# Stores of split weights: from SyncE's DMA queue to GpSimd's

## The chip, the cores and the metric

The kernel runs as one program on one core of a Trainium2 chip. The metric is the device time of that core in microseconds (us). Three timed runs of the kernel before gave 2495.51, 2503.52 and 2504.46 us; the median is 2503.52 us. The profiled execution, a fourth one, took 2499.25 us, of which 2496.5 us are the span that the trace covers.

Engines go by their short names: PE is the matrix engine (PEld its weight loads), DVE the vector engine, ACT the scalar engine, POOL is GpSimd, SP is SyncE, which here only issues DMAs. "SPq" or "POOLq" means the instruction queue of that engine.

## The reference, cut to what matters

One layer of a decoder trunk is run on a prompt of 2048 tokens and on 8 single-token samples, model width 1024:

```python
h    = rms_norm(x) * (1 + sc1) + sh1
proj = h @ w_in                       # 1024 x 3080: q, k, v, gate z, beta, alpha, u, vb
mix  = concat(gated_delta(q, k, v), u * (W_s @ vb + b))
x    = x + g1 * (mix @ w_out)         # 1024 x 1024
h2   = rms_norm(x) * (1 + sc2) + sh2
up   = causal_dwconv(h2 @ w_up)       # 1024 x 5632
x    = x + g2 * ((silu(up[:2816]) * up[2816:]) @ w_down)   # 2816 x 1024
y    = rms_norm(x)
```

All is in float32. What counts here is that the four weight matrices w_in, w_out, w_up and w_down are each used once per block of tokens, so each is needed several times.

## The kernel before, in words

**Split weights.** Each float32 operand of a large matmul is split in two parts (`split`, L98 to L100): ACT copies it to a float32r tile (the high part), DVE subtracts that from the original (`sub_lo`, L97: the low part). `gemm_steps` makes three matmuls per pair (L119 to L121). A block of split weights is a tile of 128 x 2 x 512 (512 KB).

**Kept blocks.** `wblock` (L159) gets a tile w and, the first time that a block is needed, the raw weights. Then it splits them into w and stores w to a DRAM buffer of its own (`kept[key]`, store at L166). Each later time it loads the split block from there (L162, on POOL's queue), with no split. The first time is the first 512 tokens of the mixer (segment 0: 24 tiles of w_in with 2 blocks each, and 8 of w_out with 2) and the first third of the FFN's tokens (22 pairs of w_up with 7 blocks each, 22 rows of w_down with 2). That is 48 + 16 + 154 + 44 = 262 stores of 512 KB, 198 of them in the FFN. All further blocks are loads.

**Raw weights** come in by SP's queue: `wslab` (L153) for w_in, w_out and w_up, L1058 in `down_weights` for w_down. They share SP's queue with the stores, the w_mod slabs, the token blocks (L917, L694, L725) and the output (L1128). A tile is taken from a pool: tag "w" has 6 buffers for raw slabs and split blocks of mixer and w_down, "wb" has 6 for split blocks of w_up, and "S" has 2 for raw w_down halves and for the sums of w_up blocks. A buffer can be filled again when its last readers are done; for a split block these are the matmuls and the store.

**Mixer** (to about 1046 us): four segments of 512 tokens. Segment 0 has also the w_mod matmuls and the samples. POOL has a few memsets there.

**FFN**: three chunks of 688, 688 and 680 tokens. The loop goes over 22 pairs. `up_pair` makes seven products per pair (a Strassen-like form) and adds them: six on DVE, and on POOL `G.tensor_tensor u` (L1034) and the `add` behind it (L1035, recorded at L1009). DVE reads u next (L1007/L1009 for the last product), ACT reads the sum in the convolution (L1014), DVE finishes it (L1021). After 2 or 3 pairs (`ROUNDS`) a *down round* begins: `down_weights` fetches the rows of w_down, `down` multiplies, and DVE adds the result into xa (L1086, L1087), which frees the PSUM bank.

**Order.** Each engine and each DMA queue works through its list in order; an instruction that waits for a semaphore holds up all behind it. The lists are laid out at build time by the framework's planner, which plays the whole program with assumed durations and puts on each engine whatever can go, the earlier in the program first. So when a DMA changes its queue, all lists are laid out anew.

Of the kernel before, what the change touches and what calls it, by code (L numbers as in the profile page):

```python
# [9 lines left out]
F32 = mybir.dt.float32  # L10
# [35 lines left out]
def trunk(ctx, tc, A, O):  # L46
    nc = tc.nc
    V, S_, G, PE = nc.vector, nc.scalar, nc.gpsimd, nc.tensor
# [50 lines left out]
    def split(out_h, out_l, a, eng=None):  # L99
        S_.activation(out=out_h, in_=a, func=AF.Copy)  # L100
        sub_lo(out_l, a, out_h, eng)
# [53 lines left out]


    kept = {}

    def wblock(key, w, src=None):  # L159

        if key in kept:
            G.dma_start(out=w, in_=kept[key])  # L162
        else:
            split(w[:, 0], w[:, 1], src)
            kept[key] = dr.tile([128, 2, 512], F32, name="kept_" + "_".join(map(str, key)))
            nc.sync.dma_start(out=kept[key], in_=w.bitcast(F32))  # L166
        return [(w[:, 0, k * 128:(k + 1) * 128], w[:, 1, k * 128:(k + 1) * 128]) for k in range(4)]

    def wpt():
# [2 lines left out]
    def weight(name, i):  # L172

        raw = None if (name, i, 0) in kept else wslab(A[name][i])
        return [p for j in range(2) for p in wblock(
            (name, i, j), wpt(), None if raw is None else raw[:, j * 512:(j + 1) * 512])]
# [788 lines left out]
    def up_weights(i):  # L965
        names = ("B11", "B21", "T1", "T2", "B22", "T3", "T4")
        block = lambda n, src=None: wblock(("w_up", i, n), wqt(), src)
        if ("w_up", i, "T4") in kept:
            return {n: block(n) for n in names}
        r1, r2 = wslab(A["w_up"][i]), wslab(A["w_up"][FT + i])  # L970
        a11, a12, a21, a22 = r1[:, 0:512], r1[:, 512:], r2[:, 0:512], r2[:, 512:]
        st = lambda: q1.tile([128, 512], F32, tag="S", name="S", bufs=2)
        s1, s2 = st(), st()
        V.tensor_tensor(out=s1, in0=a21, in1=a22, op=ALU.add)
        w = {"B11": block("B11", a11)}
        w["B21"] = block("B21", a12)
        w["T1"] = block("T1", s1)
        V.tensor_tensor(out=s2, in0=s1, in1=a11, op=ALU.subtract)
        w["T2"] = block("T2", s2)
        s4 = st()  # L980
        V.tensor_tensor(out=s4, in0=a12, in1=s2, op=ALU.subtract)
        w["B22"] = block("B22", s4)
        s3 = st()
        V.tensor_tensor(out=s3, in0=a11, in1=a21, op=ALU.subtract)
        w["T3"] = block("T3", s3)
        w["T4"] = block("T4", a22)
        return w
# [62 lines left out]
    def down_weights(i0, m):  # L1050

        w = [[] for _ in range(m)]
        for j in range(2):
            for i in range(m):
                key, raw = ("w_down", i0 + i, j), None
                if key not in kept:
                    raw = q1.tile([128, 512], F32, tag="S", name="S", bufs=2)
                    nc.sync.dma_start(out=raw, in_=A["w_down"][i0 + i][:, j * 512:(j + 1) * 512])  # L1058
                w[i] += wblock(key, wpt(), raw)
        return w  # L1060
# [136 lines left out]
    for s in range(NSEG):  # L1197
# [72 lines left out]
        if s == NSEG - 1:  # L1270
            nc.scalar.dma_start(out=O["nd_p"].rearrange("h k v -> k h v"),
                                in_=state.rearrange("p (h v) -> p h v", h=4))
# [50 lines left out]
    for ci, (c0, W) in enumerate(CB):  # L1323
# [31 lines left out]
        w = down_weights(pend[0], len(pend[1]))  # L1355
# [70 lines left out]
def build(nc, arrays):  # L1426
    A = {n: nc.dram_tensor(f"in_{n}", a.shape, F32, kind="ExternalInput").ap() for n, a in arrays.items()}
    O = {n: nc.dram_tensor(f"out_{n}", s, F32, kind="ExternalOutput").ap() for n, s in _OUTS.items()}
    with tile.TileContext(nc, schedule_with_timeline_sim=True) as tc:
        with ExitStack() as ctx:  # L1430
            trunk(ctx, tc, A, O)
# [11 lines left out]
```

## Time and profile before

| | us |
|---|---|
| median of three runs | 2503.52 |
| profiled execution | 2499.25 |
| its span | 2496.5 |
| PE busy | 2414.7 (97%) |
| DVE busy | 1713.3 (69%) |
| ACT busy | 1045.9 (42%) |
| POOL busy | 501.3 (20%) |

A row of waits reads: engine and line that waited, what ended the wait, total us, times, longest. A row of a timeline reads: start, length, engine, line, operation, output<-input, count, and in square brackets the engine's idle time before it and what ended it; no brackets means no such idle time. A row of windows has for each engine the busy us (and instructions), then the granted share of PE's clock, the busy share of the DMA engines and GB/s.

### The profile page before, as it was taken

To read this page: it belongs to the slowest core of one execution; us is meant where nothing else is said; L and a number is where in the kernel's file an instruction comes from. 1 tells how busy PE (TensorE), PEld (TensorE's weight loads), DVE (VectorE), ACT (ScalarE), POOL (GpSimd) and SP (SyncE) were. 2 spreads that over 40 slices of the span, in tenths; PEclk is the share of its full clock that TensorE was granted. 3 is DMA by queue.
4 is the path that set the end of the run, shared out by engine and by line. 5 is a ranking of instruction groups with operands and counts; after the bars stand their busy time and mean duration, and the time that the engine had idled before them with its cause. 6 is when DMAs were issued, how large, how long until landed. Compare 5 with 4: busy or idle time off the path is not lost.

```text
span 2496.5 us, 41843 instructions
## 1 busy us (share of the span) xinstructions
PE 2414.7 (97%) x15770; PEld 2240.9 (90%) x15770; DVE 1713.3 (69%) x3731; ACT 1045.9 (42%) x2128; POOL 501.3 (20%) x769
## 2 busy tenths in 40 slices
PE   7899999999999999999999999999999999999997
PEld 4798978888887878889999998999999999999997
DVE  4675668455745664799899998766655685666655
ACT  5766655456445645454444444412222242222223
POOL 0000001111201211311111112333333223333333
PEclk9999999999999999999999999999999999999998
DMA  9785787566737754888787778977777778767773
GB/s 377 243 282 170 255 306 212 153 194 202 209 113 223 222 163 143 305 327 307 280 298 295 284 287 302 319 225 237 240 228 223 223 233 296 225 212 231 227 238 116
DMA packets 224057, 600.84 MB, mean 241 GB/s; under 512 B 39345, under 2 KB 67697, under 8 KB 223345
## 3 DMA queue, kind: packets, MB, share of 16 engines
q0 software_dynamic: 84672, 308.32, 39.8%
q1 hardware_dynamic: 128672, 278.83, 31.6%
q10 hardware_dynamic: 10512, 11.04, 1.3%
q8 instruction: 124, 2.03, 0.3%
q14 instruction: 77, 0.62, 0.1%
HBM read 430.39 MB, written 167.70 MB: 240 GB/s over the span
## 4 chain that ended last, share of the span: by engine, by line
PE 75%; DVE 12%; DMA 7%; issue 3%; ACT 2%; SPq 0%; POOL 0%; ACTq 0%; DVEq 0%; POOLq 0%
PE u L119 9%; PE u L120 9%; PE u L121 9%; PE g L119 7%; PE g L120 7%; PE g L121 7%; PE d L119 6%; PE d L120 6%; PE d L121 6%; DVE acc L1021 1%; DVE cv L376 1%; DVE wb L97 1%; DVE sv L508 1%; DMA S<-in_w_down 1%; DVE TP L506 1%
## 5 line engine op out<-in xcount | busy, mean ns | idle before, releaser
L119 PE MATMUL g<-hh,w 128*128 128x512 f32 (+1 forms) x960 | 346.4, 361 | 7.7 <-ACT w L100 7.7
L1021 DVE SCALAR_TENSOR_TENSOR acc<-raw,vec,acc 128x680 f32<-128x680 f32 (+1 forms) x264 | 303.5, 1152 | 70.0 <-ACT acc L1014 67.6
L119 PE MATMUL d<-midh,w 128*128 128x344 f32 (+1 forms) x1008 | 322.2, 325 | 22.1 <-DVE xa L1087 11.9
L119 PE MATMUL u<-T,wb 128*128 128x344 f32 (+1 forms) x1056 | 338.1, 321 | 4.9 <-DMA wb<-kept_w_up_T 2.4
L121 PE MATMUL g<-hh,w 128*128 128x512 f32 (+1 forms) x960 | 341.6, 356 | 0.0
L120 PE MATMUL g<-hl,w 128*128 128x512 f32 (+1 forms) x960 | 340.6, 355 | 0.0
L120 PE MATMUL u<-T,wb 128*128 128x344 f32 (+1 forms) x1056 | 338.4, 321 | 0.3 <-DVE T L97 0.3
L121 PE MATMUL u<-T,wb 128*128 128x344 f32 (+1 forms) x1056 | 337.2, 320 | 0.9 <-DVE wb L97 0.9
L120 PE MATMUL d<-midl,w 128*128 128x344 f32 (+1 forms) x1008 | 323.7, 322 | 0.0
L121 PE MATMUL d<-midh,w 128*128 128x344 f32 (+1 forms) x1008 | 317.4, 322 | 0.4 <-DVE w L97 0.4
L1087 DVE SCALAR_TENSOR_TENSOR xa<-d,mod,xa 128x344 f32<-128x344 f32 (+2 forms) x368 | 206.1, 568 | 153.7 <-PE d L121 144.8
L1014 ACT ACTIVATE acc<-raw,vec 128x680 f32<-128x680 f32 (+1 forms) x132 | 125.9, 956 | 383.7 <-DVE raw L1009 379.1
L119 PE MATMUL u<-B,wb 128*128 128x344 f32 (+1 forms) x792 | 252.6, 320 | 2.7 <-ACT B L100 2.7
L120 PE MATMUL u<-B,wb 128*128 128x344 f32 (+1 forms) x792 | 253.1, 320 | 0.2
L121 PE MATMUL u<-B,wb 128*128 128x344 f32 (+1 forms) x792 | 252.0, 318 | 0.0
L162 POOL DMA_DIRECT2D w<-kept_w_in x144 | 76.2, 529 | 718.0 <-PE g L121 379.4
L119 PEld LDWEIGHTS d<-midh,w 128*128 128x128 f32 x1008 | 191.6, 191 | 26.6 <-issue 11.5
L119 PEld LDWEIGHTS g<-hh,w 128*128 128x128 f32 x960 | 182.9, 191 | 35.1 <-ACT w L100 8.6
L121 PEld LDWEIGHTS g<-hh,w 128*128 128x128 f32 x960 | 182.2, 190 | 28.1 <-issue 2.8
L120 PEld LDWEIGHTS g<-hl,w 128*128 128x128 f32 x960 | 182.9, 191 | 26.7 <-issue 2.0
L119 PEld LDWEIGHTS u<-T,wb 128*128 128x128 f32 x1056 | 199.4, 189 | 6.1 <-DVE sacc L1100 2.1
L121 PEld LDWEIGHTS u<-T,wb 128*128 128x128 f32 x1056 | 199.7, 189 | 1.3 <-DVE wb L97 1.2
(391 smaller groups left out, 5063.4 us busy)
## 6 DMA issues: line engine op xcount, KB each, us to landing
wb<-kept_w_up_T POOLq DMA_DIRECT2D x176, 512.0 KB, 5.0
w<-kept_w_in POOLq DMA_DIRECT2D x144, 512.0 KB, 4.0
wb<-kept_w_up_B POOLq DMA_DIRECT2D x132, 512.0 KB, 4.9
kept_w_up_T<-wb SPq DMA_DIRECT2D x88, 512.0 KB, 4.0
w<-kept_w_down POOLq DMA_DIRECT2D x88, 512.0 KB, 5.0
kept_w_up_B<-wb SPq DMA_DIRECT2D x66, 512.0 KB, 4.1
kept_w_in<-w SPq DMA_DIRECT2D x48, 512.0 KB, 4.2
w<-kept_w_out POOLq DMA_DIRECT2D x48, 512.0 KB, 4.4
```

Of the source, the lines that this page charges most:

```text
L97: (eng or V).tensor_tensor(out=out, in0=a, in1=hi.bitcast(F32), op=ALU.subtract)
L119: PE.matmul(ps[:, :n], wh, mh[:, c0:c0 + n], start=k == ks[0], stop=False)
L120: PE.matmul(ps[:, :n], wh, ml[:, c0:c0 + n], start=False, stop=False)
L121: pe["last"] = PE.matmul(ps[:, :n], wl, mh[:, c0:c0 + n], start=False, stop=k == ks[-1])
L162: G.dma_start(out=w, in_=kept[key])
L376: V.scalar_tensor_tensor(out=acc, in0=cr[:, j:j + SEG], scalar=vc("cqkv", ft * 4 + j), in1=acc, op0=ALU.mult, op1=ALU.add)
L506: V.tensor_tensor(out=tmp, in0=NB[:, j, j + 1:32].unsqueeze(2).to_broadcast([64, r, w]), in1=TB[:, j:j + 1, 0:w].to_broadcast([64, r, w]), ...
L508: V.tensor_tensor(out=TB[:, j + 1:32, 0:w], in0=TB[:, j + 1:32, 0:w], in1=tmp, op=ALU.subtract)
L1014: S_.activation(out=acc[:, off:W], in_=raw[:, 2:2 + m], func=AF.Identity, scale=vc("cffn", ft * 3 + 2), bias=vc("cffb", ft))
L1021: V.scalar_tensor_tensor(out=acc[:, off:W], in0=raw[:, j:j + m], scalar=vc("cffn", ft * 3 + j), in1=acc[:, off:W], op0=ALU.mult, op1=ALU.add)
L1087: V.scalar_tensor_tensor(out=xa[ft][:, b0 + o:b0 + n], in0=ps[:, o:n], scalar=mod[:, 40 + ft, 0:1], in1=xa[ft][:, b0 + o:b0 + n], op0=ALU. ...
```

## The change

The store in `wblock` goes to the queue named in a small dictionary, and that names POOL (`G = nc.gpsimd`) throughout. Raw loads stay on SP, kept loads on POOL.

```diff
     kept = {}
+    keeper = {"q": G}
 
     def wblock(key, w, src=None):
 
@@
         else:
             split(w[:, 0], w[:, 1], src)
             kept[key] = dr.tile([128, 2, 512], F32, name="kept_" + "_".join(map(str, key)))
-            nc.sync.dma_start(out=kept[key], in_=w.bitcast(F32))
+            keeper["q"].dma_start(out=kept[key], in_=w.bitcast(F32))
```

## Rows read from the trace of the kernel before

**Rows 1.** Page: span, and shares of the chain that ended last.
```profile
span 2496.5 us, 41843 instructions
...
PE 75%; DVE 12%; DMA 7%; issue 3%; ACT 2%; SPq 0%; POOL 0%; ACTq 0%; DVEq 0%; POOLq 0%
```

**Rows 2.** Windows: most of segment 0, and the FFN's first chunk (PE, PEld, DVE, ACT, POOL).
```profile
1046.00:1505.00 459.00, 441.04 (x2742) 436.88 (x2741) 429.03 (x866) 208.75 (x336) 61.09 (x43) 0.98 0.81 299
...
60.00:290.00 230.00, 217.36 (x1962) 201.79 (x1960) 154.79 (x453) 155.90 (x390) 0.00 (x0) 0.97 0.69 235
```

**Rows 3.** Waits of PE, 1046 to 1510 us.
```profile
PE d L119 <- DVE xa L1087: 9.9, 6, 2.4
PE d L119 <- ACT w L100: 3.5, 2, 2.4
```

**Rows 4.** Waits of PE, whole run: before the second chunk.
```profile
PE d L119 <- ACT midh L100: 6.0, 2, 5.0
```

**Rows 5.** Waits of PE, 60 to 330 us.
```profile
PE g L119 <- ACT w L100: 7.7, 1, 7.7
```

**Rows 6.** Timeline of ACT at the end of that wait.
```profile
90.12 1.13 ACT L100 ACTIVATE w<-wr 128x512 fp32r<-128x512 f32 x2
```

**Rows 7.** Waits of SP's queue, whole run.
```profile
SPq L166 <- DVE w L97: 179.2, 63, 13.4
...
SPq L166 <- DVE wb L97: 134.6, 91, 3.8
```

**Rows 8.** Timeline of SP's queue, 1300 to 1345 us.
```profile
1305.08 0.32 SPq L166 DMA_DIRECT2D kept_w_up_B<-wb  x1
...
1326.26 0.32 SPq L166 DMA_DIRECT2D kept_w_down<-w  x1
1326.67 0.44 SPq L1058 DMA_DIRECT2D S<-in_w_down  x1
```

**Rows 9.** Waits of ACT, 1046 to 1510 us.
```profile
ACT wb L100 <- PE u L121: 60.2, 40, 4.3
ACT w L100 <- DMA S<-in_w_down: 52.3, 31, 3.3
...
ACT wb L100 <- DMA kept_w_up_B<-wb: 0.5, 1, 0.5
```

**Rows 10.** Instructions on tile kept_w_up_T: ns min/median/max, first and last start.
```profile
L162 POOL DMA_DIRECT2D wb<-kept_w_up_T x176: 527/530/580, 1508.3 to 2443.7; - x176
L166 SPq DMA_DIRECT2D kept_w_up_T<-wb x88: 319/320/1352, 1046.3 to 1505.8; - x88
```

**Rows 11.** Timeline of POOL, one pair of the first chunk.
```profile
1303.23 1.27 POOL L1034 TENSOR_TENSOR mc<-mc 128x344 f32<-128x344 f32 x1 [32.62 <-ACT mc L1033]
1304.46 1.38 POOL L1009 TENSOR_TENSOR raw<-mc 128x344 f32<-128x344 f32 x1
```

**Rows 12.** Timeline of DVE, same pair.
```profile
1301.46 0.69 DVE L97 TENSOR_TENSOR wb<-S,wb 128x512 fp32r<-128x512 f32 x1
...
1303.64 1.41 DVE L97 TENSOR_TENSOR wb<-S,wb 128x512 fp32r<-128x512 f32 x1
1304.97 1.59 DVE L1021 SCALAR_TENSOR_TENSOR acc<-raw,vec,acc 128x680 f32<-128x680 f32 x1
1306.48 0.15 DVE L1007 TENSOR_TENSOR nfs<-u,mc 128x8 f32<-128x8 f32 x1
```

**Rows 13.** Timeline of ACT, same pair.
```profile
1307.28 0.94 ACT L1014 ACTIVATE acc<-raw,vec 128x680 f32<-128x680 f32 x1
```

**Rows 14.** L1021 in the first chunk: ns min/median/max.
```profile
L1021 DVE SCALAR_TENSOR_TENSOR acc<-raw,vec,acc x83: 906/915/1599, 1075.6 to 1504.3; 128x680 f32<-128x680 f32 x83
```

**Rows 15.** Timeline of DVE, one pair of the second chunk.
```profile
1721.53 3.65 DVE L1021 SCALAR_TENSOR_TENSOR acc<-raw,vec,acc 128x688 f32<-128x688 f32 x2 [0.85 <-ACT acc L1014]
```

**Rows 16.** L1021 in the second chunk.
```profile
L1021 DVE SCALAR_TENSOR_TENSOR acc<-raw,vec,acc x88: 921/935/2692, 1562.8 to 1992.8; 128x688 f32<-128x688 f32 x88
```

**Rows 17.** DMA issues: queue, count, size, median us from issue to landing.
```profile
wb<-kept_w_up_T POOLq DMA_DIRECT2D x176, 512.0 KB, 5.0
...
kept_w_up_T<-wb SPq DMA_DIRECT2D x88, 512.0 KB, 4.0
```

## The prediction

> **What bounds the kernel now.** I read the page first, then windows by stage, then the waits of PE in each stage, then the timelines of the queues that the change touches. The chain that ended last is PE for 75%, DVE for 12% and DMA for 7%; SP's and POOL's own queues have 0% [rows 1]. So neither the queue that is relieved nor the one that is loaded stands on the path by itself. They can act only through what they hold up.
>
> The stores run in two places. In segment 0 of the mixer (60 to 290 us) PE is busy 217.4 of 230 us and POOL not at all. In the FFN's first chunk (1046 to 1505 us) PE is busy 441 of 459 us and DVE 429 of 459, so there two engines are nearly full and PE loses only 18 us; POOL is busy 61 us [rows 2]. Of these 18 us, 13.4 lie where a down round begins: 9.9 us wait for the DVE addition into xa that frees a PSUM bank, 3.5 us for ACT's half of a w_down split [rows 3]. At the change to the second chunk PE waits once more, 5.0 us, for ACT's midh [rows 4]. All that a better order of DMAs could give back in the FFN is therefore 18 + 5 = 23 us, 0.9% of the run.
>
> In the mixer the one long wait of PE in reach is 7.7 us before a split of w_in [rows 5]. That split on ACT has no idle time ahead of it [rows 6]: ACT was busy with other work and the raw slab was there, so an earlier load would not move it.
>
> **The change part by part.**
>
> *What goes from SP.* SP's queue stood 179 us in front of stores that waited for DVE's half of a split in w, and 135 us for one in wb [rows 7]. This looks like much, but what is behind such a store? In a down round the queue shows it: the store leaves at 1326.26 us, the next raw load of w_down at 1326.67 us [rows 8]. That load fills one of two S buffers, and the buffer is free only when the same split has read it. Without the store, the load would wait for the same DVE instruction by itself. What goes is the store's issue, 0.41 us a load. From the start of a round to its third block there are two such links, 0.8 us. ACT waits 52 us for raw w_down, in 31 pieces [rows 9], but only 3.5 us of PE's waits end with that split [rows 3]; the others end with DVE, which has a full list there. I take 2 us off, between 0 (DVE is late anyway) and 13.4 us (all round starts come in time). The 64 stores in the mixer: I take 0, since the one wait there isn't for a load [rows 6]; the bound of a gain is that wait, 7.7 us.
>
> *What comes to POOL.* A DMA that POOL issues keeps it busy for 0.53 us, against 0.32 us on SP [rows 10]. 64 x 0.53 = 34 us in segment 0 lie on an empty engine: no cost. 198 x 0.53 = 105 us in the first chunk come to 61 us: 166 of 459 us, no bound. But POOL now waits for each split, and behind a waiting store stand the two additions of each pair. In the pair at 1303 us they start at 1303.23 us and end at 1305.84 us [rows 11]. DVE reads the first one's result at 1306.48 us [rows 12], where it had ended at 1304.50 us, and ACT the second one's at 1307.28 us [rows 13]: a slack of 2.0 and 1.4 us. A store that was already free before (0.53 us) is inside this slack. 22 pairs x 0.53 = 11.7 us is the upper bound for a store that goes first each time and finds no slack; with the slack of the rows I take 1 us.
>
> *What DVE loses beside POOL.* While POOL adds, DVE is longer: L97 takes 1.41 us instead of 0.69 and L1021 1.59 us [rows 12] instead of 0.915 [rows 14], together 1.4 us in this pair. In the second chunk, where POOL issues loads all the time and its additions run back to back, two L1021 take 3.65 us [rows 15] instead of 2 x 0.935 [rows 16], 1.8 us. If the first chunk becomes like the second, that is 0.4 us more a pair, 22 x 0.4 = 9 us of DVE time. PE waits for DVE only at round starts, about one pair in three, so 3 us reach the end. The bounds are -3 us (the additions come to lie beside less DVE work) and 9 us.
>
> *The stores themselves.* POOL's loads of this size land in 5.0 us, SP's stores in 4.0 [rows 17]; a store on POOL isn't in the trace. A split block's buffer is free when its matmuls and its store are done; now ACT waits 60 us for the matmuls and 0.5 us for a landing [rows 9]. So the matmuls are last and cover the store; I take 0.5 us for a landing that is 1 us later; the bound is 1 us at each of those 40 waits on ACT, of which a quarter, 10 us, would reach PE.
>
> *The change to the second chunk.* The first loads of kept w_up blocks and the last 6 stores of w_down now stand in one queue; each store adds 0.53 us, and one may wait for a split. I take 1 us, from -5 us (PE's wait there goes) to +6 us (all of it, twice).
>
> One rule speaks against the change. POOL's loads in the later chunks take 527 to 580 ns with DVE busy beside them [rows 10], so nothing holds up POOL's issue of a DMA there. The Trainium skill, page "SBUF — State Buffer", section "SBUF: two separate sides", says that a DMA issued from GpSimd stands still while certain copies on DVE lock the port through which its descriptors are written. By that rule the stores, issued while DVE is busiest, would be held up for some of DVE's instructions; this is the third rival below.
>
> **Sum.** -2 + 0 + 1 + 3 + 0.5 + 1 = 3.5 us. On the profiled execution, 2499.25 us, that gives 2502.7 us. The median of the runs is 4.3 us above that execution, so I predict 2507 us.
>
> **The rivals.**
>
> *Faster: rounds start in time.* With loads no longer in order with the stores, the planner may put the w_down splits earlier in the lists of ACT and DVE, and the waits at the round starts go. For it: ACT's 31 waits for raw w_down [rows 9]. Against it: two S buffers, and DVE 93% busy. With 13.4 us gone: 2490 us.
>
> *Slower: POOL's additions behind a store that isn't ready.* The place is POOL's queue in each pair. In the pair shown, the next store leaves SP at 1305.08 us [rows 8], after the additions. If the planner puts that store ahead of them, they begin at 1305.08 + 0.53 = 1305.6 instead of 1303.23 us, 2.4 us late; less the slack of 1.4 us, ACT's L1014 and the convolution behind it are 1.0 us late. 22 pairs make 22 us, on DVE and ACT with DVE nearly full: 2526 us. It decides as soon as the planner expects the split before PE's sixth product in most pairs. For it: the lists are made with assumed durations. Against it: in the order of time, as the trace has it, the store comes 1.9 us after.
>
> *Slower: stores held up at issue.* If each of 198 issues were held for one L1021 (0.92 us), POOL would be busy 166 + 182 = 348 of 459 us, and the additions would be 0.9 us late in each pair, 20 us in all: 2524 us. Against it: 580 ns is the longest of 176 loads [rows 10].
>
> **Chances.** My forecast, the queues hardly matter: 0.57, by itself 2494 to 2517 us. Rounds in time 0.20; additions late 0.19; issues held 0.04. A run within 0.5% of 2503.5 us (2491 to 2516 us) can't be told from no change. Faster by more than that: 0.20 for most of the first rival and a bit of the forecast's edge. Slower: 0.23 for the two rivals and 0.04 for the forecast's upper edge, so 0.27. The same: 0.53. The range goes from 2488 us, which leaves out the outer part of the first rival, to 2529 us, past both slow rivals with some of what isn't known of the new lists.
>
> **What would show it.** Right: SP's waits at L166 gone and those at L1058 and L153 grown in their place; PE's waits at the round starts near 13 us; 0.53 us a store on POOL; DVE's L1021 in the first chunk with a maximum over 2 us. Rival one: those PE waits under 5 us. Rival two: POOL's additions start over 1 us after ACT's copy, and DVE or ACT wait for them. Rival three: stores on POOL well over 0.6 us. Wrong altogether: a change of PE's waits in the mixer, or over 10 us at the seams between the stages.

## The result, and the profile after

With all stores on POOL's queue the kernel takes 2517.9 us (median of 5 runs, 2513.8 to 2518.5), beside 2502.3 us for the kernel before (5 runs). The estimated ratio is 1.0069, 95% interval 1.0057 to 1.0082 (the two medians by themselves give 1.0062): slower by 0.6 to 0.7%. In the code after, all lines from 158 on have a number one higher (the store is L167, the load of w_down L1059, the addition into xa L1088).

The page of the kernel after, its span and the first line of its section 4, the chain that ended last:

```profile
span 2512.9 us, 41962 instructions
...
PE 65%; DVE 15%; DMA 10%; issue 5%; ACT 4%; POOL 1%; SPq 0%; DVEq 0%; ACTq 0%; POOLq 0%
```

PE's share fell by 10 points against [rows 1], and DVE, DMA, ACT and the issue of instructions took it. POOL's queue has 0%, but that doesn't clear it: a store's issue counts as POOL, its landing as DMA. Followed through the trace, this chain goes through issues of stores for 4.9 us and through their landings for 14.2 us. Whether POOL's queue brings them onto the path is a question for the experiments. Where the time is lost, the windows tell (the columns of [rows 2]; the mixer's segment 0, then the FFN's first chunk):

```profile
60.00:290.00 230.00, 216.66 (x1956) 201.11 (x1955) 153.06 (x453) 156.06 (x387) 27.75 (x52) 0.98 0.68 232
1046.00:1505.00 459.00, 429.50 (x2635) 423.99 (x2634) 409.34 (x836) 199.19 (x322) 155.06 (x221) 0.97 0.77 288
```

The mixer is as it was. In the first chunk PE and DVE are both less busy than in [rows 2], by 11.5 and 19.7 us, and fewer matmuls fall into the window. Both wait more. POOL is busy 155 us instead of 61, far from full.

From PE's transpose of the row `rtok` that opens the chunk (1053.5 us, before 1056.8) to the matmul that ends PE's wait for midh before the second chunk (1540.1 us, before 1525.3) it takes 486.6 us instead of 468.5: 18.1 us more, which is all of the loss. What lies behind it took 972.8 us instead of 971.2. Two terms make up the 18 us. PE's waits of over 0.2 us in this stretch went from 22.0 to 33.6 us, 11.6 us more. And from 1046 us to 10 us past that matmul, TensorE was granted 1.2 GHz instead of 2.4 for 37.5 us instead of 23.9; PE worked in 33.1 and 20.5 us of these, and half of the difference, 6.3 us, is lost by the slower clock. PE's waits, against [rows 3]:

```profile
PE d L119 <- DVE xa L1088: 19.1, 7, 5.5
PE d L121 <- DVE w L97: 3.0, 3, 1.3
...
PE d L119 <- ACT midh L100: 1.1, 2, 0.9
```

So at the starts of the down rounds PE waits twice as long for DVE's addition into xa. And DVE is not late because it has more to do. Its own waits in the same window, first of the kernel before, then of the one after (us in total, times, longest):

```profile
DVE w L97 <- ACT w L100: 2.1, 5, 0.8
...
DVE wb L97 <- ACT wb L100: 0.2, 1, 0.2
```

```profile
DVE w L97 <- ACT w L100: 16.0, 9, 2.5
DVE wb L97 <- ACT wb L100: 10.7, 9, 3.2
```

DVE stands 26.7 us in front of splits whose ACT half isn't there, where it stood 2.3 us. One round shows how. First DVE after, from the second w_down split of the round to the first addition into xa (start, duration, line, operation, in brackets the idle time before it and what ended it):

```profile
1403.67 0.69 DVE L97 TENSOR_TENSOR w<-S,w 128x512 fp32r<-128x512 f32 x1
1404.28 0.87 DVE L1047 TENSOR_TENSOR acc<-acc 128x688 f32<-128x688 f32 x1
...
1405.14 0.51 DVE L1010 TENSOR_TENSOR raw<-u,mc 128x344 f32<-128x344 f32 x1
1408.18 0.69 DVE L97 TENSOR_TENSOR w<-S,w 128x512 fp32r<-128x512 f32 x1 [2.53 <-ACT w L100]
...
1408.86 0.87 DVE L97 TENSOR_TENSOR midl<-acc,midh 128x688 fp32r<-128x688 f32 x1
1409.69 0.93 DVE L1022 SCALAR_TENSOR_TENSOR acc<-raw,vec,acc 128x680 f32<-128x680 f32 x1
1410.53 0.69 DVE L97 TENSOR_TENSOR w<-S,w 128x512 fp32r<-128x512 f32 x1
...
1413.42 0.68 DVE L97 TENSOR_TENSOR w<-S,w 128x512 fp32r<-128x512 f32 x1
...
1414.10 0.56 DVE L1088 SCALAR_TENSOR_TENSOR xa<-d,mod,xa 128x336 f32<-128x336 f32 x1
```

ACT after, and the matmul that the addition releases:

```profile
1403.01 0.63 ACT L100 ACTIVATE w<-S 128x512 fp32r<-128x512 f32 x1 [2.49 <-DMA S<-in_w_down]
1407.51 0.64 ACT L100 ACTIVATE w<-S 128x512 fp32r<-128x512 f32 x1 [3.87 <-DMA S<-in_w_down]
1408.05 0.76 ACT L100 ACTIVATE midh<-acc 128x688 fp32r<-128x688 f32 x1
1408.71 0.94 ACT L1015 ACTIVATE acc<-raw,vec 128x680 f32<-128x680 f32 x1
```

```profile
1414.80 0.40 PE L119 MATMUL d<-midh,w 128*128 128x344 f32 x1 [3.48 <-DVE xa L1088]
```

ACT's third copy of a w_down half stands ahead of midh and of the convolution's first term (L1015). ACT is idle for 3.87 us until the raw load lands, and both of these wait with it although their inputs are there: DVE had written midh's by 1405.2 us and L1015's by 1405.7 us. DVE stands 2.53 us before the third split, with midl and L1022 behind it. In the kernel before, four splits stood ahead of the first addition into xa in each three-row round, and the third behind midl and L1021; in the kernel after, from the second three-row round on (1263 us), five stand ahead of it, and the third ahead of midl. The planner put the splits earlier in both lists. Against that stand the raw loads (DMA issues of the first chunk, before and then after; the last number is the median in us from issue to landing):

```profile
S<-in_w_down SPq DMA_DIRECT2D x41, 256.0 KB, 3.9
```

```profile
S<-in_w_down SPq DMA_DIRECT2D x38, 256.0 KB, 3.4
```

The median fell, and the mean over all 44 loads hardly did (4.38 us before, 4.30 after). The loads that ACT stands for did not get faster: in the same four rounds the third took 4.2 to 5.2 us before and 4.5 to 5.1 us after, the fourth 3.9 to 4.3 and 4.6 to 7.4 us. The third load of the round shown was issued at 1402.37 us, 0.03 us after the split that freed its S buffer, and ACT had it 5.14 us later. The chain that ended last goes through this very load (start, length, what):

```profile
1402.37 5.12 DMA S<-in_w_down
```

From 1040 to 1552 us it goes through raw loads of w_down for 38.8 us, where it was 21.0 us before.

### The profile page after: what moved, and what is told of

Read it like the earlier page. It is cut to its first block, busy times and chain, and to the rows that moved or that the text cites. A ratio compares the mean times of both kernels' runs of the same rounds, so it can differ in the third digit from the quotient of the medians.

```text
span 2512.9 us, 41962 instructions
## 1 busy us (share of the span) xinstructions
PE 2417.6 (96%) x15770; PEld 2244.4 (89%) x15770; DVE 1709.2 (68%) x3731; ACT 1047.5 (42%) x2128; POOL 643.7 (26%) x1031
## 4 chain that ended last, share of the span: by engine, by line
PE 65%; DVE 15%; DMA 10%; issue 5%; ACT 4%; POOL 1%; SPq 0%; DVEq 0%; ACTq 0%; POOLq 0%
PE u L119 7%; PE u L120 7%; PE u L121 7%; PE g L119 7%; PE g L121 7%; PE g L120 7%; PE d L119 5%; PE d L121 5%; PE d L120 5%; DVE acc L1022 2%; DVE wb L97 2%; DMA S<-in_w_down 2%; DMA wr<-in_w_up 1%; DMA nd<-nz 1%; DVE sv L509 1%
## 5 line engine op out<-in xcount | busy, mean ns | idle before, releaser
L1022 DVE SCALAR_TENSOR_TENSOR acc<-raw,vec,acc 128x680 f32<-128x680 f32 (+1 forms) x264 | 305.2, 1159 | 69.9 <-ACT acc L1015 67.3
L1088 DVE SCALAR_TENSOR_TENSOR xa<-d,mod,xa 128x344 f32<-128x344 f32 (+2 forms) x368 | 206.4, 568 | 158.1 <-PE d L121 147.9
L1015 ACT ACTIVATE acc<-raw,vec 128x680 f32<-128x680 f32 (+1 forms) x132 | 126.0, 956 | 396.8 <-DVE raw L1010 386.8
L119 PEld LDWEIGHTS u<-T,wb 128*128 128x128 f32 x1056 | 199.7, 189 | 9.2 <-DVE mc L1028 2.6
L120 PEld LDWEIGHTS u<-T,wb 128*128 128x128 f32 x1056 | 200.0, 189 | 0.1
L121 PEld LDWEIGHTS u<-T,wb 128*128 128x128 f32 x1056 | 200.1, 190 | 0.0
```

The costliest lines, as they stand in the source:

```text
L119: PE.matmul(ps[:, :n], wh, mh[:, c0:c0 + n], start=k == ks[0], stop=False)
L120: PE.matmul(ps[:, :n], wh, ml[:, c0:c0 + n], start=False, stop=False)
L121: pe["last"] = PE.matmul(ps[:, :n], wl, mh[:, c0:c0 + n], start=False, stop=k == ks[-1])
L1015: S_.activation(out=acc[:, off:W], in_=raw[:, 2:2 + m], func=AF.Identity, scale=vc("cffn", ft * 3 + 2), bias=vc("cffb", ft))
L1022: V.scalar_tensor_tensor(out=acc[:, off:W], in0=raw[:, j:j + m], scalar=vc("cffn", ft * 3 + j), in1=acc[:, off:W], op0=ALU.mult, op1=ALU.add)
L1088: V.scalar_tensor_tensor(out=xa[ft][:, b0 + o:b0 + n], in0=ps[:, o:n], scalar=mod[:, 40 + ft, 0:1], in1=xa[ft][:, b0 + o:b0 + n], op0=ALU. ...
```

## Experiments

Two theories stood against each other. **The lists:** the loss comes from the new order of the engines' instructions, not from the stores. **The queue:** it comes from POOL issuing and landing the stores, or from what then waits on POOL. The table has all twelve runs and the two kernels, with what the profile of each says of the first chunk. "w" and "acc" are DVE's waits for ACT's half of a w_down split and for the convolution's first term, "xa" is PE's wait for DVE's addition, all in us between 1046 and 1510 us; "round" is the mean time from one round to the next, by the first addition into xa, over the last four three-row rounds of this window. Each of these four columns is read from one profiled execution.

| run | stores on POOL | lists | ratio to before (95%) | w | acc | xa | round |
|---|---|---|---|---|---|---|---|
| before | none | before | 1 | 2.1 | 1.4 | 9.9 | 65.4 |
| after | all | after | 1.0069 (1.0057, 1.0082) | 16.0 | 0.8 | 19.1 | 68.1 |
| e1_held_after | all | new, 2 splits held | 1.0058 (1.0038, 1.0078) | 14.6 | 0.8 | 15.1 | 67.9 |
| e2_fifth_before | none | new, xa held | 1.0067 (1.0046, 1.0089) | 3.7 | 4.6 | 24.1 | 68.5 |
| e3_up_only | w_up | new | 1.0014 (0.9997, 1.0031) | 5.4 | 0.3 | 13.5 | 65.5 |
| e4_down_only | w_down | new | 1.0061 (1.0043, 1.0080) | 17.0 | 1.1 | 21.0 | 68.5 |
| f1_pool_old_lists | all | before | 1.0025 (1.0007, 1.0043) | 3.5 | 1.4 | 11.8 | 64.8 |
| f2_sync_new_lists | none | after | 1.0094 (1.0079, 1.0109) | 14.7 | 1.0 | 16.9 | 68.2 |
| f3_pool_old_dve | all | DVE before | 1.0083 (1.0069, 1.0097) | 0.5 | 12.9 | 17.4 | 67.1 |
| f4_sync_new_dve | none | DVE after | 1.0144 (1.0129, 1.0159) | 19.7 | 1.2 | 21.7 | 69.6 |
| g1_pool_old_act_dve | all | ACT, DVE before | 1.0008 (0.9989, 1.0026) | 2.4 | 1.4 | 10.9 | 65.0 |
| g2_pool_old_act | all | ACT before | 1.0052 (1.0033, 1.0070) | 9.3 | 0.8 | 13.5 | 65.9 |
| g3_mixer_only | mixer's | new | 0.9993 (0.9980, 1.0007) | 3.5 | 2.0 | 13.0 | 65.2 |
| g4_early_rounds_sync | none | new, 3 splits held | 0.9994 (0.9980, 1.0007) | 3.0 | 1.2 | 6.9 | 64.6 |

The length of the first chunk, measured as above from the transpose of `rtok` to the end of PE's wait for midh, parts the runs in two groups: 463.7 to 472.0 us in before, e3, f1, g1, g3 and g4, and 476.9 to 492.1 us in the other eight, which are those with a ratio of 1.005 or more.

### One part of the stores at a time: e3, e4, g3

```diff
-            nc.sync.dma_start(out=kept[key], in_=w.bitcast(F32))
+            (G if key[0] in ("w_up",) else nc.sync).dma_start(out=kept[key], in_=w.bitcast(F32))
```

e4 names "w_down" in this place, g3 "w_in" and "w_out".

> Only the 154 stores of w_up blocks go out on POOL; those of w_in, w_out and w_down stay on SP. DVE's list keeps four w_down splits ahead of the first addition in the later rounds. List theory: about the kernel before, 2498 to 2508 us. POOL theory: 154 of the 198 stores in the first chunk, so about three quarters of the loss, 2511 to 2516 us. Additions of POOL behind stores (the slower rival of the prediction): 1 us a pair, 2515 to 2525 us.

> Only the 44 stores of w_down blocks go out on POOL; all others stay on SP. DVE's list then has five w_down splits ahead of the first addition in the later rounds, as in the changed kernel. List theory: most of the loss, 2510 to 2520 us. POOL theory: 44 of 198 stores, under a quarter of the loss, 2502 to 2507 us.

> Only the 64 stores of w_in and w_out go to POOL, the FFN's 198 keep SP. Theory of the lists: the mixer has no wait that ends with them, no change, 2497 to 2505 us, unless the FFN's lists change with it (ACT's differs from before in 139 places, some of them in the FFN): then as much as its rounds get longer. If the mixer's stores cost something by themselves: the window from 60 to 290 us has PE at 215 us or less, and 2506 us or more.

The 154 stores of w_up cost nothing that the interval can tell, though they are more than three quarters of the FFN's stores and stand beside POOL's additions; the mixer's 64 cost nothing; the 44 of w_down bring nearly all of the loss. The theory of the queue can't say why 44 stores should weigh more than 154. The lists can: on SP's queue a store of w_down stands directly ahead of each round's third to sixth raw load of w_down (as in [rows 8]), stores of w_up only ahead of the first two. In e3 DVE's list has the second split earlier, ahead of the multiplication L1046, and DVE waits 5.4 us for w; in e4, from the second three-row round on, five splits stand ahead of the first addition, and it waits 17.0 us.

### The place of single splits: e1, e2, g4

e1, on the kernel after, holds the fifth and the sixth w_down split of a three-row round on DVE behind the third and the fifth addition into xa (of a two-row round, the fourth behind the third addition). g4, on the kernel before, does it with the last three, behind the third, fifth and seventh. The lines of e1 that do it:

```diff
-                    cur["w"] = down_weights(pend[0], len(pend[1]))
+                    i0, m = pend[0], len(pend[1])
+                    todo = [(j, i) for j in range(2) for i in range(m)]
+                    now = m + 1 if ci == 0 else 2 * m
+                    cur["w"] = down_weights(i0, m, todo[:now])
+                    added.clear()
                     down(cur["w"], pend[1], W, off, xa, halves=(0,))
+                    for t, e in zip(todo[now:], (2, 4)):
+                        with tc.issue_after(added[e].ins):
+                            down_weights(i0, m, [t], cur["w"])
```

e2, on the kernel before, puts the first four additions behind DVE's split of the fifth block.

```diff
+            fifth = halves == (0,) and b0 == 0 and subs[0] and len(mids) > 2
+            with tc.issue_after(subs[4].ins) if fifth else ExitStack():
...
```

> All 262 stores stay on POOL, as in the changed kernel. In the first chunk's down rounds of three rows, DVE's split of the fifth w_down block is ordered behind the third addition into xa, and the sixth behind the fifth addition, as DVE's list had it before the change; in the changed kernel five splits stand ahead of the first addition, before it four. List theory (the loss of about 16 us comes from that one more split ahead of the additions that free PSUM): the time comes back to the kernel before, 2497 to 2507 us, and PE's waits at the round starts fall from 3.5 us each to about 2. POOL theory (the loss comes from the stores that wait in POOL's queue, land later and hold up POOL's additions): no change against the changed kernel, 2513 to 2521 us.

> All stores stay on SP, as in the kernel before. In the down rounds of three rows the additions into xa of the first four products are ordered behind DVE's split of the fifth w_down block, as the changed kernel has it. List theory: slower than before by most of the loss, 2509 to 2522 us, PE's waits at round starts 3.5 us or more. POOL theory: within 3 us of the kernel before, 2499 to 2506 us.

> The queues as before; in each round of the first chunk with three rows DVE makes only three w_down splits ahead of the additions into xa, and the other three behind the third, fifth and seventh. If DVE's in-order wait for the fourth split (0.8 us and the 0.7 us of the split itself) is what keeps PE waiting at the start of a round: PE's waits for xa fall from about 2 to under 1 us a round, with less time at the half clock, 2488 to 2497 us. If the fourth split only comes late elsewhere (the second half of the round then waits for it, or the S buffers come free later): no change, 2498 to 2506 us, with new waits of PE for ACT's or DVE's half of w.

e2 shows that an order alone, with no store moved, can cost as much as the change. e1 was a miss for my theory in its first form, that the fifth split makes the loss: with it held, the loss stayed. In e1 the second and third splits are still early, and DVE still waits 14.6 us for them. g4 took PE's waits for xa down to 6.9 us, as hoped, and the time did not move. In its profile the first chunk is 463.7 us long instead of 468.5 and a round 64.6 us instead of 65.4, but the chunk begins at 1063.6 us instead of 1056.8; over the profiles of this case that start lies anywhere from 1051.7 to 1065.7 us, so one execution can't settle 5 us. What takes back the shorter waits stays open. It is no version that beats the kernel before.

### Queues and lists apart: f1, f2

The two programs have the same instructions but for the queue of the stores. So each engine's list can be written down from one program and imposed on the other, by edges that fix the order alone and add no wait:

```diff
+        for a, b in zip(order, order[1:]):
+            tc.add_manual_dep(byname[b], a, mybir.DependencyInfo(
+                mybir.DependencyClass.NoSync, mybir.DependencyReason.DATA), reason="follow")
```

> All 262 stores on POOL's queue, but PE, DVE, ACT, POOL's additions and SP's loads keep, instruction by instruction, the order of the kernel before; only the place of the stores among POOL's additions is new. Theory of the lists (the loss comes from the new order of DVE's, ACT's and PE's instructions in the FFN's first chunk): no loss, 2498 to 2506 us beside about 2501 for the kernel before; DVE waits about 2 us in chunk 1 for ACT's half of a w_down split (changed kernel 16.0), PE about 10 us for xa. Theory of the queue (POOL issues and lands the stores later, or its additions come late): the loss stays, 2512 to 2519 us, whatever the lists are.

> All stores on SP's queue as before, but PE, DVE, ACT, POOL's additions and SP's loads in the order of the changed kernel. Theory of the lists: the whole loss appears with no store moved, 2511 to 2519 us, DVE waits 12 us or more in chunk 1 for ACT's half of the splits and PE 15 us or more for xa. Theory of the queue: as before, 2498 to 2506 us.

The traces show that the lists were followed: in f1 all of DVE's 3731 and ACT's 2128 instructions come in the order of the kernel before, in f2 all of DVE's in the order of the kernel after. With the lists before and all stores on POOL the time is 2503.4 us beside 2498.3, and the first chunk takes 466.8 us. With the lists after and no store moved it is 2522.5 us, the chunk 485.8 us: the whole loss, and a little over, without a single store on POOL. The chain that ended last says the same of the stores: in f1 it goes through no issue and no landing of one, in f2 through landings for 16.7 us with all of them on SP's queue (after: 14.2). So it is the order of the lists, not POOL's queue, that puts stores on the chain in these two. DVE's waits in f1 and then in f2:

```profile
DVE w L97 <- ACT w L100: 3.5, 7, 0.9
```

```profile
DVE w L97 <- ACT w L100: 14.7, 15, 2.4
```

One round of f1, DVE from the second split to the first addition, ACT beside it, and PE:

```profile
1395.18 0.68 DVE L97 TENSOR_TENSOR w<-S,w 128x512 fp32r<-128x512 f32 x1
...
1396.21 0.86 DVE L97 TENSOR_TENSOR midl<-acc,midh 128x688 fp32r<-128x688 f32 x1
...
1397.37 0.93 DVE L1022 SCALAR_TENSOR_TENSOR acc<-raw,vec,acc 128x680 f32<-128x680 f32 x1 [0.23 <-ACT acc L1015]
1399.15 0.69 DVE L97 TENSOR_TENSOR w<-S,w 128x512 fp32r<-128x512 f32 x1 [0.85 <-ACT w L100]
...
1402.09 0.68 DVE L97 TENSOR_TENSOR w<-S,w 128x512 fp32r<-128x512 f32 x1
...
1403.46 0.55 DVE L1088 SCALAR_TENSOR_TENSOR xa<-d,mod,xa 128x336 f32<-128x336 f32 x1
```

```profile
1393.45 0.63 ACT L100 ACTIVATE w<-S 128x512 fp32r<-128x512 f32 x1 [2.59 <-DMA S<-in_w_down]
1395.22 0.78 ACT L100 ACTIVATE midh<-acc 128x688 fp32r<-128x688 f32 x1 [1.14 <-DVE acc L1047]
1396.38 0.96 ACT L1015 ACTIVATE acc<-raw,vec 128x680 f32<-128x680 f32 x1 [0.38 <-DVE raw L1010]
1398.49 0.63 ACT L100 ACTIVATE w<-S 128x512 fp32r<-128x512 f32 x1 [1.15 <-DMA S<-in_w_down]
```

```profile
1404.16 0.40 PE L119 MATMUL d<-midh,w 128*128 128x344 f32 x1 [2.25 <-DVE xa L1088]
```

The third raw load took as long here, 5.46 us from its issue at 1393.03 us to ACT's copy. But midh and L1015 on ACT, midl and L1022 on DVE stand ahead of the third split and fill part of the load's time; DVE waits 0.85 us instead of 2.53. From the second split to the first addition it is 8.3 us here and 10.4 us in the kernel after.

### Which list: f3, f4, g1, g2

The same edges, for DVE's list alone (f3, f4), for ACT's and DVE's (g1), for ACT's alone (g2); the planner lays the others out anew around them.

> All stores on POOL; only DVE's list is held to the order before, PE, ACT, POOL and SP are laid out anew around it. If DVE's order alone makes the loss (splits of the second, third and fifth w_down block too early): 2498 to 2506 us. If PE's or ACT's new order has a share of its own, between that and 2517: 2508 to 2514. Theory of the queue: 2512 to 2519 us.

> All stores on SP; only DVE's list is that of the changed kernel, the others are laid out anew around it. DVE's order alone: 2511 to 2519 us. PE's or ACT's order has a share: 2504 to 2511. Theory of the queue: 2498 to 2506 us.

> All stores on POOL; ACT's and DVE's lists are held to the order before, PE, POOL and SP are laid out anew around them. If the loss comes from ACT and DVE standing in front of w_down splits whose raw loads have not landed: it is gone, 2498 to 2507 us, some 65 us from one round to the next as before (changed kernel 68). If PE's new order has a share of its own: 2508 to 2516 us.

> All stores on POOL; only ACT's list is held to the order before; DVE's is laid out anew around it and has four splits ahead of the first addition into xa, the second of them one place earlier than before. If ACT's copy that stands too early is what makes the loss (it holds up midh and the convolution's first term, for which DVE waited 2.65 us in the kernel where DVE's list alone was the old one): 2498 to 2507 us. If DVE's splits of the second and third block make it by themselves: 2511 to 2518 us.

f3 refuted that DVE's order alone makes the loss. With DVE's old list DVE no longer waits for w; ACT now does the standing for it. In f3's round ACT's third copy is ahead of L1015, and DVE waits for L1015 instead, 12.9 us in all (ACT, then DVE):

```profile
1346.43 0.63 ACT L100 ACTIVATE w<-S 128x512 fp32r<-128x512 f32 x1 [2.28 <-DMA S<-in_w_down]
1346.97 0.94 ACT L1015 ACTIVATE acc<-raw,vec 128x680 f32<-128x680 f32 x1
```

```profile
1347.95 0.93 DVE L1022 SCALAR_TENSOR_TENSOR acc<-raw,vec,acc 128x680 f32<-128x680 f32 x1 [2.65 <-ACT acc L1015]
```

g2 is the other half: with ACT's old list and DVE's new one DVE waits 9.3 us for w again, and 0.5% is lost. With both old (g1) nothing is lost, although PE's list, POOL's and SP's are the planner's new ones and all stores are on POOL. So holding one of the two lists is not enough to take the loss away, and holding both takes away all that the interval can tell. f4, DVE's new list beside an ACT list made for SP's stores, is the worst of all: my expectation for it, at most 2519 us, was too low by 13 us.

## Why the prediction was right in its range and wrong in its cause

The forecast was "the queues hardly matter", 2507 us, "by itself 2494 to 2517 us". The time of 2517.9 us lies just outside that and inside the whole range, 2488 to 2529 us. That the range holds is in the main luck: it reaches that far on the slow side for two rivals, and neither was the cause. Of the queues themselves the forecast was about right (f1, g1). What it missed is the lists, and its own sign says so: PE's waits at the round starts were to stay near 13 us and came to 19.4 us (19.1 for xa, 0.3 for w).

**The step that failed** is the first term, *what goes from SP*: 2 us off, "between 0 (DVE is late anyway) and 13.4 us". It had no bound on the side of a loss. The runs show in its place a loss of 18 us in the first chunk (after), of 17 us with the lists alone (f2), and about nothing when ACT and DVE keep their order (g1, 1.0008). The saving itself came as worked out: a load now leaves SP 0.03 us after the split that frees its buffer instead of 0.44 us. But beside it the planner's new lists have the splits ahead of work that had covered the load's landing.

**The first rival** named this very mechanism, splits earlier in ACT's and DVE's lists, and gave it only the sign of a gain. The rows to see that it can lose were there: ACT's 52 us of waits for raw w_down [rows 9] said that the loads are late by the plan already, and an in-order engine that is moved closer to a late load stands longer.

**The other terms.** *SP:* its waits at the store are gone, and those at the loads have grown, as forecast, against [rows 7]:

```profile
SPq L1059 <- DVE nfs L1008: 107.1, 4, 27.5
SPq L153 <- PE d L121: 81.4, 11, 14.3
SPq L1059 <- DVE wb L97: 58.9, 8, 26.7
```

*POOL and the rival of late additions* (0.19): DVE waits for POOL's additions 2.1 us in the whole chunk, in two waits, and ACT not at all. That rival is out for the change. What the queue costs by itself is 0.08% in g1 (at most 0.26%) and 0.25% in f1 (0.07 to 0.43%), so a few us may be POOL's; the times of these two runs don't settle it, and the first chunk of f1's profile, 466.8 us, has no room for them. *The stores held up at issue* (0.04) and *DVE beside POOL's additions* are read from these rows of the chunk (ns: shortest, median, longest):

```profile
L1022 DVE SCALAR_TENSOR_TENSOR acc<-raw,vec,acc x80: 907/918/2389, 1071.2 to 1486.3; 128x680 f32<-128x680 f32 x80
```

```profile
L167 POOL DMA_DIRECT2D kept_w_up_T<-wb x82: 531/531/571, 1047.7 to 1503.9; - x82
L167 POOL DMA_DIRECT2D kept_w_up_B<-wb x61: 531/531/573, 1046.4 to 1501.0; - x61
L167 POOL DMA_DIRECT2D kept_w_down<-w x38: 531/531/573, 1096.8 to 1483.6; - x38
```

No issue of a store in the chunk took over 573 ns, with DVE busy 89% of the time beside them; the longest of all 262 took 728 ns, once, in the mixer. The Trainium skill, page "SBUF — State Buffer", section "SBUF: two separate sides", lets DVE copies of a certain kind stall a DMA that GpSimd issues; no run here shows that. L1022 has a maximum over 2 us, as the sign said, but that is a single instruction. The next longest takes 1.6 us, as in [rows 14], the median is 918 ns beside 915, and no L1022 of g1's first chunk takes over 1.6 us. So the 3 us of this term are not there, and that its sign came is luck.

*The mixer* was priced at 0, and g3 has 0.9993. *The landing* was priced at 0.5 us; in the chunk, the stores of w_up landed in 4.7 us (T blocks) and 4.1 us (B) on POOL against 4.0 [rows 17] and 4.1 on SP, those of w_down in 4.4 against 3.0. What of that reaches the end can't be told from g1's 0.08%. *The seam* to the second chunk: PE waits 5.7 us there instead of 5.0 [rows 4], within the 1 us that I took.

What isn't shown: why the planner moved the splits. It plays the program with durations of its own, and no trace has them. That it expects the loads sooner when no store stands between them is inferred from e3 and e4 (only the stores of w_down matter).

## What to carry to other kernels

Where a planner lays out in-order engines, moving a DMA to another queue is a change of every engine's list, and the lists can cost more than the queues: put a loss as well as a gain beside it, and compare the lists before the times. To tell the two apart, impose the old order on the new program and the new order on the old one. Look first for work that now stands behind a wait for a load: what covered the landing before (midh, L1014 and midl here) must stay ahead of it.

## What was unexpected in the hardware

The clock doesn't follow from the length of the wait in these runs. Before, a wait of 2.38 us for xa was followed by a stretch with a granted clock of 0.56, most of it at the 1.2 GHz level (first window, the eighth column); after, the wait of 3.48 us shown above was followed by 1.00, at 2.4 GHz (second window).

```profile
1403.20:1406.60 3.40, 3.40 (x13) 3.40 (x14) 2.83 (x7) 1.28 (x3) 0.00 (x0) 0.56 0.58 187
```

```profile
1414.80:1418.20 3.40, 3.40 (x22) 3.40 (x23) 3.40 (x10) 1.38 (x2) 0.66 (x2) 1.00 0.69 277
```

Over the chunk more waiting went together with more time at 1.2 GHz: 27.3 to 47.8 us of it in the eight slower runs of the table, 6.8 to 23.9 us in the other six (each from 1046 us to 10 us past the end of PE's wait for midh). So a few us of wait in each round cost more than themselves, here 6.3 us on top of 11.6; which single wait is followed by it can't be read from these rows.
